# Candidate stages ahead of the dense chunks, stored split panels and stride-4 gate matmuls in a one-core encoder block

## The chip, the core and the metric

The kernel runs on one core of one Trainium2 chip. The metric is the device time of one execution in microseconds (us), lower is better. The time before is 3102.21 us, the median of 3 runs (3095.23 to 3104.54).

## What is computed

One residual block over 1024 tokens of width 1024, in f32. A mixer with 8 softmax heads and 8 stick-breaking heads comes first, then a PEER layer: every token picks, for each of 8 heads, 16 of 16384 single-neuron experts by product keys, and sums their outputs.

```python
query = (ht @ w_query).reshape(t, PEER_HEADS, 2, PEER_HALF)
sub_scores = jnp.einsum('thpd,hpkd->thpk', query, sub_keys)
half_vals, half_idx = lax.top_k(sub_scores, PEER_TOPK)
cand = (half_vals[:, :, 0, :, None] + half_vals[:, :, 1, None, :]).reshape(t, PEER_HEADS, 256)
top_vals, top_pos = lax.top_k(cand, PEER_TOPK)
experts = i1 * PEER_N_KEYS + i2
gates = jax.nn.softmax(top_vals, axis=-1)
...
act = jax.nn.gelu(jnp.einsum('td,thkd->thk', xb, expert_down[eb])) * gb
y = jnp.einsum('thk,thkd->td', act, expert_up[eb])
```

## The kernel before, in words

The 8 token tiles (128 tokens each) form two blocks. Block A holds tiles 0 to 4, block B tiles 5 to 7. The program has two parts.

**The front** runs, for both blocks, the projections, the attention, and then three steps. `post` (L774) is the output projection with w_out, `post_b` the second norm and transpose, and `route` (L825) the query projection with w_q and the top 16 of each half. Matrix products with f32 accuracy are done with split operands: a weight panel of 128x1024 is split into a high part (`wh`, ScalarE, L336) and a low part (`wl`, VectorE, L342), and `mm3` (L353) issues three matmuls for each piece. The class `Panels` (L316) loads a panel (L328), splits it and hands it out. `post` and `route` take 8 panels of w_out and 16 of w_q: 24 for block A, and the same 24 again for block B. The generator `cands` (L907) makes from eight rows of top-16 lists the final experts and gates. It is a chain of small VectorE operations with 12 yields; block A has five such stages, block B three (they are collected in `b.rest`).

The 5 tiles of block A are computed **densely**: all 16384 experts for all tokens, multiplied by a gate matrix that is zero except at the chosen experts. For tiles 0 and 1 the gate matrix is made by GpSimd: `scatter` (L1004) issues 256 indirect DMAs that add 128 gates each into the DRAM tensors `gds` (one for each of the two tiles, in turn). For tiles 2 to 4 it is made by TensorE: `gbuild` (L1016) builds one-hot tiles (VectorE L1033 and L1046, ScalarE L1042), multiplies them (L1050, 768 matmuls of 128x128), evicts them on ScalarE (L1052, 96 times) into `gt`, and stores that to DRAM as `gd` (L1055).

**The dense part** (from L1226) runs 32 groups of 4 chunks of 128 experts. A chunk's down panel is split (`split_d`), multiplied (`gelu_s`, L1274), passed through Gelu (L1280) and multiplied by its gates (`mul_g`, L1282); then the group's up products run into 10 accumulators. The gates of a group are loaded by `loadg` (L1248) from `gds` and `gd`; for the first two groups these loads stand on GpSimd's queue.

The 3 tiles of block B are computed **sparsely** beside it: the generator `sparse` (L1181) first runs the three `cands` stages of block B (36 steps), then for each expert slot gathers 128 rows of `expert_down` or `expert_up` into one of 5 `ring` buffers with an indirect DMA on GpSimd (L1194, L1207) and multiplies them on VectorE (L1196, L1212). `pump(n)` advances this generator by n steps at fixed places of the dense loop; `PUMP_0` is how many steps are issued ahead of the first `split_d`.

The order: in the front a scheduler sets each engine's order from the program and a timing model. In the dense part VectorE, ScalarE and TensorE run in the order in which the code is written; the order on GpSimd and on SP, which issues all plain DMAs, is still the scheduler's.

Of the kernel before, what the change touches and what calls it, by code (L numbers as in the profile page):

```python
# [11 lines left out]
F32 = mybir.dt.float32  # L12
F32R = mybir.dt.float32r
# [3 lines left out]
AF = mybir.ActivationFunctionType  # L17
# [3 lines left out]
P = 128  # L21
T = 1024
D = 1024
# [24 lines left out]
O2B = 2  # L48
WB = 3
UB = 4  # L50
PUMP_0 = 7
PUMP_C = 2
PUMP_U = 5
PUMP_V = 2
# [51 lines left out]
def tile_kernel(ctx: ExitStack, tc: tile.TileContext, x, ccol, w_ada, badac, bgt2, gcols, w_in, w_f, bf_, gout,  # L106
                w_out, w_q, keysT, edown, eup, wdense, gfin, out, dbg=None, stop=None):
    nc = tc.nc
    V, S, G, PE = nc.vector, nc.scalar, nc.gpsimd, nc.tensor
    dma = nc.sync.dma_start  # L110
# [3 lines left out]
    dram = ctx.enter_context(tc.tile_pool(name="dram", bufs=1, space=bass.MemoryType.DRAM))  # L114
# [38 lines left out]
    qsp = dram.tile([8, 3, P, T], F32R, name="qsp")  # L153
    ksp = dram.tile([8, 2, P, T], F32R, name="ksp")
    vsp = dram.tile([8, P, T], F32, name="vsp")
    gd = dram.tile([NPT * P // SB, P, NE * SB], F32, name="gd")
    gds = [dram.tile([NE * P * P, 1], F32, name="gds%d" % i) for i in range(NSC)]
    pidx = cst.tile([P, 1], F32, name="pidx")
# [2 lines left out]
    class Block:  # L161
        def __init__(self, t0, parts):
            self.t0, self.parts = t0, []
            i0 = 0
            for n in parts:
                self.parts.append((i0, n))
                i0 += n
            self.nt = i0
            self.ht = i0 * P
            self.nk = (t0 + i0) * P  # L170
            self.nq = 2 if t0 else 1
# [67 lines left out]
    def defer(fn, n=1):  # L239
        t_ = [n, fn]  # L240
        late.append(t_)
        return t_

    def force(t_):
        if t_ in late:
            late.remove(t_)
            t_[1]()
# [27 lines left out]
    def mrg(*streams, bg=()):  # L275
        live = [[q[0], float(q[1]), 0.0, q[2] if len(q) > 2 else 0] for q in streams + tuple(bg)]
        side = [q[0] for q in bg]
        need = len(streams)
        while need:
            for q in sorted(live, key=lambda q: q[2] / q[1]):  # L280
                c = adv(q)
                if c is None or c >= 0:
                    break
            assert c is None or c >= 0
            if c is None:
                live.remove(q)
                need -= not any(q[0] is g for g in side)
                continue
            q[2] += c
            tick(c)  # L290
            step()
        while late:
            late.pop(0)[1]()
        lead.clear()
# [17 lines left out]
    def split(dst_h, dst_l, src):  # L312
        S.activation(dst_h, src, AF.Copy)
        V.tensor_sub(dst_l, src, dst_h.bitcast(F32))

    class Panels:  # L316
        def __init__(self, pool, srcs, bufs=3, eng=V):
            self.eng = eng
            self.pool, self.src, self.bufs = pool, list(srcs), bufs
            self.ld, self.sp = [], []  # L320
            for _ in range(bufs - 1):
                self.load()
            self.split()

        def load(self):
            if self.src:
                w = self.pool.tile([P, D], F32, name="wf", tag="wf", bufs=self.bufs)
                dma(w, self.src.pop(0))  # L328
                self.ld.append(w)

        def split(self):
            if self.ld:
                w = self.ld.pop(0)
                wh = self.pool.tile([P, D], F32R, name="wh", tag="wh", bufs=2)
                wl = self.pool.tile([P, D], F32R, name="wl", tag="wl", bufs=2)
                S.activation(wh, w, AF.Copy)  # L336

                def low():
                    if self.eng is G:
                        G.tensor_sub(wl, w, wh.bitcast(F32))  # L340
                    else:
                        V.tensor_sub(wl, w, wh.bitcast(F32))  # L342

                self.sp.append((wh, wl, defer(low, LW)))
                self.load()

        def get(self):
            wh, wl, t_ = self.sp.pop(0)
            force(t_)
            self.split()  # L350
            return wh, wl

    def mm3(pt, wh, wl, hh, hl, cs, m=P, k0=0, k1=KD):  # L353
        for kd in range(k0, k1):
            c = slice(kd * m, (kd + 1) * m)
            PE.matmul(pt, wl[:, c], hh[:, kd, cs], start=kd == 0, stop=False)  # L356
            PE.matmul(pt, wh[:, c], hl[:, kd, cs], start=False, stop=False)  # L357
            PE.matmul(pt, wh[:, c], hh[:, kd, cs], start=False, stop=kd == KD - 1)  # L358
# [657 lines left out]
    def gbuild(ti, gp, alloc):  # L1016
        tp = alloc()
        for n, s_ in enumerate(cols3[ti]):
            PE.transpose(tp[:, n * P:(n + 1) * P], s_, identf)
        ib = gp.tile([P, 2, P], BF, name="ib", tag="ib", bufs=2)  # L1020
        S.activation(ib, tp[:, :2 * P].rearrange("p (n t) -> p n t", n=2), AF.Copy)
        gT = gp.tile([P, P], F32, name="gT", bufs=2)
        S.activation(gT, tp[:, 2 * P:3 * P], AF.Copy)
        io4 = gp.tile([P, P, 4], BF, name="io4", bufs=1)
        if ti == NSC:
            V.tensor_copy(io4, iof[:, :, None].to_broadcast([P, P, 4]))
            gio.append(io4)
        iob = gio[0][:, None].to_broadcast([P, 2, P, 4])

        def onehot(n, t):  # L1030
            o = gp.tile([P, 2, P, 4], BF, name="ob%d" % n, tag="ob", bufs=3)
            ids = ib[:, n, t:t + 8].rearrange("p (q t) -> p q t", t=4)[:, :, None, :]
            V.tensor_tensor(o, iob, ids.to_broadcast([P, 2, P, 4]), OP.is_equal)  # L1033
            return o.rearrange("p q i t -> p q t i")

        for sb in range(P // SB):
            gt = gp.tile([P, NE, SB], F32, name="gt", tag="gt", bufs=GTB)
            for q in range(SB // 8):
                t = sb * SB + q * 8
                e2 = onehot(1, t)  # L1040
                o2 = gp.tile([P, 2, 4, P], F32, name="o2", tag="o2", bufs=O2B)
                S.activation(o2, e2, AF.Copy)  # L1042
                e1 = onehot(0, t)
                o1 = gp.tile([P, 2, 4, P], F32, name="o1", tag="o1", bufs=O1B)
                gs = gT[:, t:t + 8].rearrange("p (q t) -> p q t", t=4)[:, :, :, None]
                V.tensor_tensor(o1, e1, gs.to_broadcast([P, 2, 4, P]), OP.mult)  # L1046
                for q2 in range(2):
                    pg = alloc()
                    for r in range(4):
                        PE.matmul(pg[:, r * P:(r + 1) * P], o2[:, q2, r], o1[:, q2, r], start=True, stop=True)  # L1050
                    c_ = q * 8 + q2 * 4
                    S.activation(gt[:, :, c_:c_ + 4].rearrange("p i t -> p t i"), pg.rearrange("p (t i) -> p t i", i=P),  # L1052
                                 AF.Copy)
                    yield GBC
            dma(gd[(ti - NSC) * (P // SB) + sb], gt.rearrange("p i t -> p (i t)"))  # L1055

# [2 lines left out]
    st_hpa, st_pw, st_hpb, st_xp, st_ad, st_at, st_s3, st_gp = [ExitStack() for _ in range(8)]  # L1059

    def pool(stack, name, bufs=1, **kw):
        return stack.enter_context(tc.tile_pool(name=name, bufs=bufs, reuse_waits="tile", **kw))
# [8 lines left out]
    def xtile(p_, b, name):  # L1071
        return p_.tile([P, b.nt, D], F32, name=name, tag="xr")
# [35 lines left out]
    am[0], ax[0] = ALS[0]()  # L1108
    s3p = pool(st_s3, "s3p", side="right")
    wop = [w_out[j] for j in range(KD)] + [w_q[j] for j in range(16)]  # L1110
    opan = Panels(s3p, wop, bufs=2)
    mrg((post(bA, mixA, lambda: xtile(xp, bA, "x1A"), opan), 60, HPB), (ad3, AD3), bg=((pp, PP3), (zr, ZR3)))
    rA = chain(post_b(bA), route(bA, opan))
    mrg((pp, PP4), (ad5, 10), bg=((rA, TOT_RA, HPC), (zr, 20)))
    for st_ in (st_ad, st_hpb, st_pw, st_xp):
# [8 lines left out]
    am[0], ax[0] = ALS[2]()  # L1124
    soft_rs[0] = RS2
    mb = pool(st_at, "mb")
    opan = Panels(s3p, wop, bufs=2)
    hp_[0] = pool(st_hpa, "hpc", 2)
    gp = pool(st_gp, "gp")
    mrg((chain(post(bB, mixB, lambda: xtile(mb, bB, "x1B"), opan), post_b(bB), route(bB, opan)), 150),  # L1130
        (chain(*[gbuild(ti, gp, ptp) for ti in range(NSC, ND)]), TOT_G))
    for st_ in (st_gp, st_hpa, st_at, st_xp, st_s3):
        st_.close()
# [192 lines left out]
    def sp_(n):  # L1326
        pump(n)
# [4 lines left out]
    def nextload():  # L1332
        i1 = next(loads, None)
        if i1 is not None:
            ready.append(load(i1))

    for _ in range(WB):
        nextload()
    sp_(PUMP_0)
    nxt = ready.pop(0)  # L1340
# [103 lines left out]
```

## Time and profile before

| | |
|---|---|
| median of 3 runs | 3102.21 us (3095.23 to 3104.54) |
| the profiled execution, its own time | 3110.21 us |
| its span | 3108.4 us |
| TensorE busy | 2856.6 us, 92% |
| VectorE busy | 2562.2 us, 82% |
| ScalarE busy | 1213.7 us, 39% |
| GpSimd busy | 1605.1 us, 52% |
| mean granted TensorE clock | 0.965 |
| HBM read, written | 721.52 MB, 77.76 MB |

Busy times are sums over the whole span, and an engine's share is an average over stages that differ. Times in the trace are counted from the span's start, and L12 is line 12 of the kernel before. PE is TensorE, DVE VectorE, ACT ScalarE, POOL GpSimd, and SP the engine that issues plain DMAs. A line that names a wait gives the idle time just before an instruction and what ended it; a row of a view of waits gives who waited for whom, the total, how often, and the longest.

### The profile page before, as it was taken

What the parts mean: (1) busy time and instruction counts of PE and PEld (TensorE: products, weight loads), DVE (VectorE), ACT (ScalarE), POOL (GpSimd) and SP (SyncE); (2) the same over time, 40 slices, a digit from 0 to 9 for tenths busy, and PEclk for the clock granted to TensorE, in tenths of its full rate; (3) what the DMA queues carried; (4) which work ended last, traced back from release to release, by engine and by line L of the source; (5) the groups of instructions that cost most, each with busy time, mean ns of one, the idle gap of its engine ahead of it and who ended that gap; (6) DMA issues with size and microseconds to landing.
All of it is one profiled execution on the core that took longest, in us unless ns stands there. A gap on an engine that the chain in (4) does not pass through costs nothing.

```text
span 3108.4 us, 47296 instructions
## 1 busy us (share of the span) xinstructions
PE 2856.6 (92%) x17213; PEld 2642.6 (85%) x17213; DVE 2562.2 (82%) x5226; ACT 1213.7 (39%) x2098; POOL 1605.1 (52%) x1092
## 2 busy tenths in 40 slices
PE   5899998998988895379999999999999999999997
PEld 4899998988888794379989989899898988999986
DVE  6677655899987697388988999899899988989986
ACT  5566645446677873131222213222122231222312
POOL 0000000077777666426566776665676756657771
PEclk9999999998989998689999999999999999999999
DMA  7999433455535555449999999999999999999995
GB/s 251 287 343 280 135 125 120 138 126 135 123 66 129 157 154 138 92 149 342 357 338 336 343 343 334 353 338 356 328 349 346 336 347 347 349 337 330 351 326 191
DMA packets 360313, 802.43 MB, mean 258 GB/s; under 512 B 66168, under 2 KB 174736, under 8 KB 358544
## 3 DMA queue, kind: packets, MB, share of 16 engines
q0 software_dynamic: 150352, 413.34, 39.4%
q1 hardware_dynamic: 209728, 386.08, 36.6%
q8 instruction: 135, 2.21, 0.3%
q14 instruction: 98, 0.80, 0.1%
HBM read 721.52 MB, written 77.76 MB: 257 GB/s over the span
## 4 chain that ended last, share of the span: by engine, by line
PE 29%; POOL 19%; issue 19%; DMA 17%; DVE 12%; ACT 2%; SPq 0%; POOLq 0%; DVEq 0%; ACTq 0%
POOL gds L1012 7%; DMA gds<-g,e 7%; POOL ring L1194 6%; DMA ring<-in_eup,e 6%; POOL ring L1207 5%; PE sp L356 3%; PE sp L357 3%; PE sp L358 3%; DMA wa<-in_w_ada 2%; PE po L1303 2%; PE po L1304 2%; PE po L1305 2%; PE proj L356 2%; PE proj L357 2%; PE proj L358 2%
## 5 line engine op out<-in xcount | busy, mean ns | idle before, releaser
L356 PE MATMUL sp<-hT,dl 128*128 128x320 f32 x2048 | 636.0, 311 | 86.3 <-ACT ge L1280 77.5
L1207 POOL DMA_INDIRECT ring<-in_eup,e x384 | 578.9, 1508 | 256.5 <-DVE sacc L1212 172.4
L1194 POOL DMA_INDIRECT ring<-in_edown,e x384 | 503.9, 1312 | 394.5 <-DVE ring L1196 230.8
L1012 POOL DMA_INDIRECT gds<-g,e x256 | 471.4, 1841 | 321.0 <-DVE i L867 136.4
L357 PE MATMUL sp<-hT,dh 128*128 128x320 f32 x2048 | 635.3, 310 | 0.0
L358 PE MATMUL sp<-hT,dh 128*128 128x320 f32 x2048 | 635.3, 310 | 0.0
L1212 DVE SCALAR_TENSOR_TENSOR sacc<-ring,sdot,sacc 128x1024 f32<-128x1024 f32 x381 | 489.3, 1284 | 56.0 <-DMA ring<-in_eup,e 51.4
L1196 DVE SCALAR_TENSOR_TENSOR ring<-ring,sx 128x1024 f32<-128x1024 f32 x384 | 460.9, 1221 | 67.9 <-DMA ring<-in_edown,e 67.0
L356 PEld LDWEIGHTS sp<-hT,dl 128*128 128x128 f32 x2048 | 386.9, 189 | 88.7 <-ACT ge L1280 79.9
L1269 ACT ACTIVATE uh<-wfu 128x1024 fp32r<-128x1024 f32 x128 | 134.8, 1053 | 672.5 <-PE po L1305 672.5
L357 PEld LDWEIGHTS sp<-hT,dh 128*128 128x128 f32 x2048 | 386.9, 189 | 1.2
L358 PEld LDWEIGHTS sp<-hT,dh 128*128 128x128 f32 x2048 | 386.7, 189 | 0.0
L1303 PE MATMUL po<-ul,ch 128*128 128x512 f32 x768 | 302.6, 394 | 17.5 <-DVE accB L1312 10.1
L1280 ACT ACTIVATE ge<-sp 128x320 f32<-128x320 f32 x256 | 110.5, 433 | 499.4 <-PE sp L358 492.6
L1304 PE MATMUL po<-uh,ch 128*128 128x512 f32 x768 | 300.6, 391 | 0.0
L1305 PE MATMUL po<-uh,cl 128*128 128x512 f32 x768 | 300.3, 391 | 0.0
L1304 PE MATMUL pers<-uh,ch 128*128 128x512 f32 x512 | 199.6, 390 | 0.0
L1303 PE MATMUL pers<-ul,ch 128*128 128x512 f32 x512 | 199.5, 390 | 0.0
L1305 PE MATMUL pers<-uh,cl 128*128 128x512 f32 x512 | 199.2, 389 | 0.0
L302 POOL TENSOR_TENSOR i<-ms,mhalf 128x4 f32<-128x4 f32 (+1 forms) x16 | 22.4, 1400 | 331.0 <-DVE ms L300 331.0
L1303 PEld LDWEIGHTS po<-ul,ch 128*128 128x128 f32 x768 | 145.1, 189 | 53.8 <-DVE accB L1312 16.0
L1305 PEld LDWEIGHTS po<-uh,cl 128*128 128x128 f32 x768 | 145.2, 189 | 30.5
(306 smaller groups left out, 6519.4 us busy)
## 6 DMA issues: line engine op xcount, KB each, us to landing
wfd<-in_wdense SPq DMA_DIRECT2D x128, 512.0 KB
wfu<-in_wdense SPq DMA_DIRECT2D x128, 512.0 KB
wa<-in_w_ada SPq DMA_DIRECT2D x96, 256.0 KB
wf<-in_w_in SPq DMA_DIRECT2D x48, 512.0 KB
gd<-gt SPq DMA_DIRECT2D x12, 2048.0 KB
g<-gd SPq DMA_DIRECT2D x30, 768.0 KB
gds<-zt SPq DMA_DIRECT2D x32, 512.0 KB
wf<-in_w_q SPq DMA_DIRECT2D x32, 512.0 KB
```

The costliest lines, as they stand in the source:

```text
L356: PE.matmul(pt, wl[:, c], hh[:, kd, cs], start=kd == 0, stop=False)
L357: PE.matmul(pt, wh[:, c], hl[:, kd, cs], start=False, stop=False)
L358: PE.matmul(pt, wh[:, c], hh[:, kd, cs], start=False, stop=kd == KD - 1)
L1012: G.indirect_dma_start(out=gds[i], out_offset=off, in_=b.g[:, c_:c_ + 1], in_offset=None, compute_op=OP.add)
L1194: G.indirect_dma_start(out=r, out_offset=None, in_=edown, in_offset=bass.IndirectOffsetOnAxis(ap=bs.e[:, c_:c_ + 1], axis=0))
L1196: (V.scalar_tensor_tensor(r, r, 1.0, sx, op0=OP.mult, op1=OP.mult, accum_out=s_[:, j:j + 1]))
L1207: G.indirect_dma_start(out=r, out_offset=None, in_=eup, in_offset=bass.IndirectOffsetOnAxis(ap=bs.e[:, c_:c_ + 1], axis=0))
L1212: (V.scalar_tensor_tensor(acc, r, s_[:, j:j + 1], acc, op0=OP.mult, op1=OP.add))
L1269: S.activation(k.uh, k.wfu, AF.Copy)
L1303: PE.matmul(po, k.ch[:, tcs], k.ul[:, ds_], start=c == 0 and (gi == 0 or not per), stop=False)
L1304: PE.matmul(po, k.ch[:, tcs], k.uh[:, ds_], start=False, stop=False)
L1305: PE.matmul(po, k.cl[:, tcs], k.uh[:, ds_], start=False, stop=c == CG - 1 and (gi == NG - 1 or not per))
```

## The change

Three edits.

1. `PUMP_0` goes from 7 to 44: all 36 candidate steps of block B and the first 8 sparse slots are issued before the first dense split.
2. Block A's `Panels` also stores each split panel (`wh` and `wl`, 512 KB each) to a DRAM tensor `wsp`; block B reads them back through a new class `Kept`, with three buffers, and neither loads nor splits its own.
3. The 128x128 gate matmuls of `gbuild` write every fourth column of their PSUM tile, so that the eviction reads and writes runs of four.

```diff
-PUMP_0 = 7
+PUMP_0 = 44
...
+    wsp = dram.tile([24, 2, P, D], F32R, name="wsp")
...
     class Panels:
-        def __init__(self, pool, srcs, bufs=3, eng=V):
-            self.eng = eng
+        def __init__(self, pool, srcs, bufs=3, eng=V, keep=None):
+            self.eng, self.keep = eng, keep and list(keep)
...
                 S.activation(wh, w, AF.Copy)
+                kp = self.keep.pop(0) if self.keep else None
 
                 def low():
                     if self.eng is G:
                         G.tensor_sub(wl, w, wh.bitcast(F32))
                     else:
                         V.tensor_sub(wl, w, wh.bitcast(F32))
+                    if kp is not None:
+                        for n_, t_ in enumerate((wh, wl)):
+                            dma(kp[n_].bitcast(F32), t_.bitcast(F32))
...
+    class Kept:
+        def __init__(self, pool, srcs, bufs=3):
+            self.pool, self.src, self.bufs, self.ld = pool, list(srcs), bufs, []
+            for _ in range(bufs - 1):
+                self.load()
+
+        def load(self):
+            if self.src:
+                src = self.src.pop(0)
+                t = [self.pool.tile([P, D], F32R, name=n_, tag=n_, bufs=self.bufs) for n_ in ("wh", "wl")]
+                for n_, t_ in enumerate(t):
+                    dma(t_.bitcast(F32), src[n_].bitcast(F32))
+                self.ld.append(t)
+
+        def get(self):
+            self.load()
+            return self.ld.pop(0)
...
                     for r in range(4):
-                        PE.matmul(pg[:, r * P:(r + 1) * P], o2[:, q2, r], o1[:, q2, r], start=True, stop=True)
+                        PE.matmul(pg.rearrange("p (i t) -> p i t", t=4)[:, :, r], o2[:, q2, r], o1[:, q2, r],
+                                  start=True, stop=True)
                     c_ = q * 8 + q2 * 4
-                    S.activation(gt[:, :, c_:c_ + 4].rearrange("p i t -> p t i"), pg.rearrange("p (t i) -> p t i", i=P),
-                                 AF.Copy)
+                    S.activation(gt[:, :, c_:c_ + 4], pg.rearrange("p (i t) -> p i t", t=4), AF.Copy)
...
-    opan = Panels(s3p, wop, bufs=2)
+    opan = Panels(s3p, wop, bufs=2, keep=[wsp[j] for j in range(24)])
...
-    opan = Panels(s3p, wop, bufs=2)
+    st_s3.close()
+    opan = Kept(pool(st_s3, "s3k", side="right"), [wsp[j] for j in range(24)], 3)
```

How the order moves. First VectorE where the dense part begins (`dl` is the low part of a down panel, `ul` of an up panel, `e` the expert numbers, rows with `bq`, `bi`, `cur` are candidate steps, `ring,sdot` a sparse slot). Before:

```order
L867 MAX_INDEX i_12774<-v_12773,sr 128x8
L865 MATCH_REPLACE sr<-v_12773,scs 128x128
L955 SCALAR_TENSOR_TENSOR bq<-pos,bq 128x128
L1264 TENSOR_TENSOR dl<-wfd,dh 128x1024 x2
L865 MATCH_REPLACE sr<-v_12773,scs 128x128
L866 MAX v_12773<-sr 128x8 x2
L1272 TENSOR_TENSOR ul<-wfu,uh 128x1024
L959 CAST bi<-af 128x128
```

With the change (its lines are 24 higher there):

```order
L1017 SCALAR_TENSOR_TENSOR tm<-af,bq 128x128
L1024 CAST e_4710<-tm 128x128
L1220 SCALAR_TENSOR_TENSOR ring,sdot<-ring,sx 128x1024 x8
L1288 TENSOR_TENSOR dl<-wfd,dh 128x1024 x2
L1296 TENSOR_TENSOR ul<-wfu,uh 128x1024
L1220 SCALAR_TENSOR_TENSOR ring,sdot<-ring,sx 128x1024 x2
L1310 TENSOR_TENSOR ge<-ge,gg 128x256
```

The first two dense splits stood in the middle of block B's first candidate stage; now they stand behind all three stages and behind eight sparse slots.

GpSimd's order is the same in both kernels. Here it is with the change, from the end of the scatters:

```order
L1035 DMA gds_108<-g_4709,e_4708 2097152x1
L1035 DMA gds_109<-g_4709,e_4708 2097152x1
L1277 DMA gg<-gds_108 128x512
L1277 DMA gg<-gds_109 128x512
...
L1279 DMA g_14191<-gd 128x12x128
L1213 DMA sx<-h2d 128x1024
L1218 DMA ring<-in_edown,e 128x1024
```

Nothing moved on this queue: the gate loads of the first two groups stand behind the last scatter, and the first sparse gather behind them.

Last, SP's queue in block A's `route`, while block B is still being projected. Before:

```order
L545 DMA ksp<-pka 128x384
L545 DMA ksp<-pkb 128x384
L328 DMA wf<-in_w_in 128x1024
L328 DMA wf<-in_w_q 128x1024
L328 DMA wf<-in_w_in 128x1024
```

With the change:

```order
L568 DMA ksp<-pka 128x384
L568 DMA ksp<-pkb 128x384
L329 DMA wf<-in_w_in 128x1024
L347 DMA wsp<-wh 128x1024
L347 DMA wsp<-wl 128x1024
L329 DMA wf<-in_w_q 128x1024
L329 DMA wf<-in_w_in 128x1024
```

Two stores of 512 KB now precede the load of each further panel. In block B's part each load of a raw panel gives way to two loads from `wsp`.

## Rows read from the trace of the kernel before

**Rows 1.** Page: TensorE by slices of 77.7 us; waits in 1210:1300 (VectorE), 1200:1300 (TensorE).

```profile
PE   5899998998988895379999999999999999999997
...
DVE ge L1286 <- DMA gg<-gds: 62.9, 1, 62.9
PE sp L356 <- ACT ge L1280: 69.8, 1, 69.8
```

**Rows 2.** GpSimd's timeline around the last scatter: start, us, engine, line, operation [idle before].

```profile
1276.34 1.55 POOL L1012 DMA_INDIRECT gds<-g,e  x1 [0.31 <-issue]
1278.20 1.55 POOL L1012 DMA_INDIRECT gds<-g,e  x1 [0.30 <-issue]
1279.90 0.63 POOL L1253 DMA_DIRECT2D gg<-gds  x1 [0.15 <-issue]
...
1285.06 0.59 POOL L1189 DMA_DIRECT2D sx<-h2d  x1
1339.73 1.04 POOL L1194 DMA_INDIRECT ring<-in_edown,e  x1 [54.08 <-DVE tv L935]
1370.69 1.55 POOL L1194 DMA_INDIRECT ring<-in_edown,e  x1 [29.92 <-DVE e L1001]
1372.55 1.95 POOL L1194 DMA_INDIRECT ring<-in_edown,e  x1 [0.30 <-issue]
1374.81 1.64 POOL L1194 DMA_INDIRECT ring<-in_edown,e  x1 [0.30 <-issue]
```

**Rows 3.** Four stretches: PE, PEld, DVE, ACT, POOL busy (count), clock, DMA share, GB/s.

```profile
624.00:797.00 173.00, 154.32 (x1000) 146.46 (x999) 169.14 (x763) 90.47 (x182) 125.11 (x70) 0.92 0.56 133
797.00:943.00 146.00, 131.16 (x914) 120.59 (x914) 131.79 (x393) 105.18 (x213) 107.59 (x60) 0.89 0.39 79
943.00:1210.00 267.00, 224.37 (x1508) 212.52 (x1507) 221.30 (x681) 203.09 (x269) 181.64 (x93) 0.95 0.57 162
1222.00:1278.00 56.00, 3.29 (x23) 3.02 (x21) 0.00 (x0) 0.00 (x0) 46.74 (x31) 0.57 0.22 0
```

**Rows 4.** GpSimd's timeline near the front's end, and its scatter waits over the whole span.

```profile
1203.09 1.61 POOL L1012 DMA_INDIRECT gds<-g,e  x1 [1.25 <-issue]
1205.00 1.55 POOL L1012 DMA_INDIRECT gds<-g,e  x1 [0.30 <-issue]
1210.71 2.70 POOL L1012 DMA_INDIRECT gds<-g,e  x1 [4.16 <-DMA gds<-g,e]
...
POOL gds L1012 <- DMA gds<-g,e: 120.8, 70, 6.1
```

**Rows 5.** Groups of instructions in 943:1210, count, then busy us and mean ns.

```profile
L1012 POOL DMA_INDIRECT gds<-g,e x93 | 183.2, 1970 | 82.2 <-DMA gds<-g,e 61.5 <-issue 20.8
L1052 ACT ACTIVATE gt<-tp 128x512 f32<-128x512 f32 x96 | 98.7, 1118 | 29.5 <-PE tp L1050 17.9 <-DMA gd<-gt 8.9 <-issue 2.5
L342 DVE TENSOR_TENSOR wl<-wf,wh 128x1024 fp32r<-128x1024 f32 x22 | 27.6, 1254 | 8.8 <-ACT wh L336 7.0 <-ACT of L809 1.6
L336 ACT ACTIVATE wh<-wf 128x1024 fp32r<-128x1024 f32 x22 | 23.3, 1058 | 0.0
L856 ACT ACTIVATE scs<-proj 128x384 f32<-128x384 f32 x16 | 8.0, 502 | 9.8 <-DVE sr L865 7.3 <-PE proj L854 1.3 <-issue 1.2
```

**Rows 6.** Splits on VectorE and panel loads in 624:797.

```profile
L342 DVE TENSOR_TENSOR wl<-wf,wh 128x1024 fp32r<-128x1024 f32 x14 | 17.2, 1226 | 0.0
...
wf<-in_w_in SPq DMA_DIRECT2D x3, 512.0 KB
```

**Rows 7.** VectorE's timeline: first and last step of one candidate stage of block B.

```profile
1304.98 0.73 DVE L923 TENSOR_TENSOR cand<-v 128x128 f32<-128x128 f32 x5
1338.13 0.23 DVE L1001 CAST e<-tm 128x128 int32<-128x128 f32 x1
```

**Rows 8.** Timeline, TensorE's first dense matmul, and ScalarE's first Gelu of groups 0, 2, 3.

```profile
1208.99 0.63 PE L356 MATMUL sp<-hT,dl 128*128 128x320 f32 x1 [7.33 <-DVE dl L1264]
...
1214.76 0.44 ACT L1280 ACTIVATE ge<-sp 128x320 f32<-128x320 f32 x1 [9.86 <-PE sp L358]
...
1419.22 0.44 ACT L1280 ACTIVATE ge<-sp 128x320 f32<-128x320 f32 x1 [4.49 <-PE sp L358]
...
1474.60 0.44 ACT L1280 ACTIVATE ge<-sp 128x320 f32<-128x320 f32 x1 [4.49 <-PE sp L358]
```

**Rows 9.** VectorE's timeline, second and third sparse slot.

```profile
1376.33 1.23 DVE L1196 SCALAR_TENSOR_TENSOR ring<-ring,sx 128x1024 f32<-128x1024 f32 x1 [0.69 <-DMA ring<-in_edown,e]
1380.76 1.23 DVE L1196 SCALAR_TENSOR_TENSOR ring<-ring,sx 128x1024 f32<-128x1024 f32 x1 [1.33 <-DMA ring<-in_edown,e]
```

**Rows 10.** TensorE's gate matmuls on the timeline, one merged run.

```profile
1102.28 1.87 PEld L1050 LDWEIGHTS tp<-o,o 128*128 128x128 f32 x16
1102.38 1.95 PE L1050 MATMUL tp<-o,o 128*128 128x128 f32 x16
```

## Prediction

> **What bounds the kernel now.** I read the slices of the page first: TensorE is 90% busy or more from the nineteenth slice (1400 us) on, and in the three before it, from 1166, only 50, 30 and 70% [rows 1]. Two limits follow, one behind the other. In the dense part it is TensorE itself: groups 2 and 3 begin 1474.60 - 1419.22 = 55.4 us apart [rows 8], and nothing in this change touches the work of a group. So a gain or a loss must show in when the dense part gets going. The waits in that hole say what it is for [rows 1]: VectorE stands 62.9 us before the first gate multiplication, for the load of `gg`, and TensorE behind it for 69.8 us. That load stands on GpSimd's queue behind the last of the 256 scatters, which is issued at 1278.20, and goes out at 1279.90 [rows 2]. So the front's engines are through by about 1210, and **the scatter chain sets the start.** Work that VectorE, ScalarE or TensorE save in the front only lengthens the hole.
>
> What paces the chain is read from four stretches [rows 3]. With no plain traffic (1222 to 1278) one scatter takes 1278.20 - 1276.34 = 1.86 us [rows 2]. At 79 GB/s it takes 146/60 = 2.43, at 133 GB/s 173/70 = 2.47, at 162 GB/s 267/93 = 2.87. How it does so stands in [rows 4]: the scatter at 1210.71 waited 4.16 us for an earlier one to land, since those to one tensor go one after another; such waits sum to 120.8 us. Traffic makes landings late. The chain is not short of work: these waits and the issue gaps are all that 943 to 1210 shows [rows 5].
>
> **The change, part by part.**
>
> *Stored panels, engines.* Block B loses 24 splits: 24 x 1.254 = 30 us of VectorE and 24 x 1.058 = 25 us of ScalarE [rows 5]. I cost both at nothing on the path: the scatters cover them, by about 70 us (1210 to 1280). The front may end some 35 us earlier.
>
> *Stored panels, traffic.* Block A writes 24 x 1.05 = 25 MB more and block B reads 12.6 MB more. Only what moves after the first scatter counts. Of the 14 splits after 624, 5 belong to block B's projection (3 loads seen, two panels in flight), so 9 are block A's [rows 6]: 9.4 MB over 173 us, +55 GB/s. How much that slows a scatter the trace shows only by its stretches, so I bound it: the flattest pair of [rows 3] (79 to 133 GB/s) gives 0.0007 us per GB/s, the steepest (0 to 162) 0.0063. I take the middle, 0.0035: 2.47 + 0.19 = 2.66 us, 65 scatters in place of 70. The 5 that are left are made up at the end at 1.86: **+9 us** (bounds +1 and +16). For block B, 12.6 MB more in 232 us in place of 267 makes (43 + 12.6)/232 = 241 GB/s; at the slope between its neighbours (79 to 162: 0.0053) a scatter takes 2.87 + 0.42 = 3.29. Then 232/3.29 = 70.5 are done there and 35/1.86 = 18.8 in the quiet 35 us that follow: 89.3 of 93, so 3.7 x 1.86 = +7. If the front ends no earlier, it is 267/3.12 = 85.6 and +14. I take **+10**; the bounds are -10 (flat slope, earlier end: 232/2.92 + 18.8 = 98.2 done) and +16. SP's queue carries the 48 stores; each waits for the same low split as the load behind it waited for before, so I add nothing for that.
>
> *Candidates ahead.* One stage takes 1338.13 + 0.23 - 1304.98 = 33 us with some dense work inside [rows 7], two and a half are left when the front ends, so about 75 us. They now run in the hole, beside the last scatters. A scatter's own issue is 1.55 us with VectorE idle [rows 2] and 1.97 on average beside a busy one [rows 5]. The last 59 us at 1.86 + 0.42 in place of 1.86 hold 26 scatters, not 32: at most +11, at least 0; I take **+5**. VectorE's lost splits could give back 0.42 x 93 x 30/221 = 5; I leave that in the lower bound.
>
> *Eight slots ahead of the first split.* These wait on VectorE for gathers that stand on GpSimd behind the last scatter, and everything dense is queued behind them; TensorE's first matmul waits for `dl`. So the two chunks that TensorE now does before the hole are no longer done ahead. Against the same last scatter: GpSimd is free at 1285.65 after `sx`; eight gathers at 1372.55 - 1370.69 = 1.86 us start until 1298.7 [rows 2]; a gather is used 1376.33 - 1372.55 = 3.8 to 1380.76 - 1374.81 = 6.0 us after its start [rows 2, 9], so the last slot begins at 1302.5 to 1304.7. With 1.2 for it and 1.2 for `dl`, TensorE starts at 1305 to 1307, and the first Gelu follows 1214.76 - 1208.99 = 5.8 us later [rows 8], at 1311 to 1313. Before, group 2 begins at 1419.22; two groups back that is 1308.4. So what the hole took before (two chunks ahead, but then candidate stages in between the chunks) and what it takes now nearly cancel: **+4 us**, between 0 and +15 (if gathers come at the 3 us at which ring buffers come free later).
>
> *Stride-4 gate matmuls.* ScalarE's eviction takes 1118 ns for 512 columns; 384 contiguous ones take 502 [rows 5], so I estimate 650 and a saving of 96 x 0.47 = 45 us (0 if the stride was not its cost). It lies before the hole: nothing. A matmul takes 1.95/16 = 0.12 us now [rows 10]; strided writes are not in this trace. In the front TensorE has 267 - 224 = 43 us free [rows 3] and the hole adds 70, so up to 113/768 = 0.15 us more for each costs nothing; with the 24 us of later scatters, 0.18. I take no loss.
>
> The sparse stream ends about 37 steps earlier; the tail then waits for TensorE's last groups as before: 0.
>
> Sum: 9 + 10 + 5 + 4 = +28 on the profiled execution's own 3110.21, so 3138. That execution lies 8 us above the median of 3102.21; against the median the forecast is **3130 us**, slower by 0.9%. Bounds: 1 - 10 - 5 + 0 = -14 and 16 + 16 + 11 + 15 = +58, so 3088 to 3160.
>
> **The rivals.** A difference of under 0.3% (9 us) cannot be told from none.
>
> *Earlier quiet, faster.* A loaded scatter costs about the same at any traffic, as 2.43 and 2.47 at 79 and 133 GB/s suggest. Then denser traffic costs nothing, and a front that ends 35 us earlier gives the chain a quiet stretch sooner: 35 us at 1.86 in place of 2.87 is 6.6 scatters, 12 us, and VectorE's lost splits give 5. With +1 and +4 the time is 3102 - 12 = 3090. It decides if traffic above 162 GB/s slows a scatter by less than 0.1 us. Against it speaks the step from 2.47 to 2.87.
>
> *A draw.* The two effects cancel, and the start costs its +4: 3095 to 3111.
>
> *Slow strided writes.* If each gate matmul took four times its 0.12 us, TensorE would get 768 x 0.37 = 281 us more; 137 of it is covered (43 + 70 + 24), and the front's end, no longer the scatters, would set the start: 3130 + 144 = 3274. It decides above 0.18 us more per matmul. The Trainium skill, page "SBUF — State Buffer", section "Door 1: The DMA port swizzle", says that any non-contiguous access to PSUM significantly slows matmuls, since a PSUM line holds two f32 values; it names no factor, and no run here shows one. By that rule at a factor of two the cover would still hide it, and at four this rival would be the result.
>
> That the change does not do what it says is excluded by the order: the three stages and eight slots do stand ahead.
>
> **How the numbers follow.** The later scatters: 0.55. The faster rival: 0.22. The draw: 0.19. Slow strided writes: 0.04. So faster 0.22, same 0.19, slower 0.59. The forecast's own range is 3112 to 3160. To hold 8 in 10 the range takes in the draw and most of the faster rival, and leaves out the strided one: 3086 to 3162.
>
> **What would show each step.** Right: the last scatter is issued later than 1278, near 1302; scatters in the stretches after 624 and after 943 at 2.6 to 3.3 us; the eight slots' waits on VectorE end just behind it, and TensorE's first dense matmul comes some 27 us after the last scatter; groups still 55.4 us apart. Wrong: a last scatter before 1270, a first dense matmul ahead of it, or group times that differ; a gate matmul run of 16 well above 1.95 us would point to the last rival.

## The result and the profile after

The changed kernel takes 3137.84 us, the median of 4 runs (3131.62 to 3143.17), against 3103.38 on the same chip: a ratio of 1.0108 [1.0085, 1.0131] (the brackets after a ratio are its 95% interval), **slower by 1.1%**. The forecast was 3130, within 3086 to 3162. The profiled execution took 3143.17 us, with a span of 3141.4; against the profiled execution before that is 33 us more.

| profiled execution | before | after |
|---|---|---|
| span, us | 3108.4 | 3141.4 |
| VectorE busy | 2562.2 | 2538.4 |
| ScalarE busy | 1213.7 | 1149.2 |
| HBM read, written, MB | 721.52, 77.76 | 734.11, 102.92 |
| last scatter issued at | 1278.20 | 1302.07 |
| first Gelu of group 2 | 1419.22 | 1450.79 |

VectorE lost 24 us of work and ScalarE 64, and the time grew. The traffic grew by the 25 MB and 12.6 MB that the prediction counted. The page's slices of TensorE (78.5 us each) show the hole that [rows 1] showed, now deeper: 10, 0 and 90% in the sixteenth to eighteenth slice, where it was 50, 30 and 70.

```profile
PE   5899998989988981099999999999999999999997
```

The waits of VectorE and TensorE in 1150:1360 (who waited for whom: us in total, times, longest) name other tiles than [rows 1]. VectorE now stands first for the first gather of the eight sparse slots, and TensorE for `dl`, the low part of the first down panel, which is queued behind those slots:

```profile
DVE ring L1220 <- DMA ring<-in_edown,e: 61.9, 4, 59.7
...
PE sp L379 <- DVE dl L1288: 140.2, 1, 140.2
```

The four stretches of [rows 3] again (PE, PEld, DVE, ACT, POOL busy with count, clock, DMA share, GB/s):

```profile
624.00:797.00 173.00, 154.47 (x1013) 146.20 (x1012) 170.02 (x770) 90.55 (x186) 113.07 (x63) 0.93 0.66 180
797.00:943.00 146.00, 131.76 (x909) 120.68 (x909) 130.23 (x380) 103.46 (x205) 108.29 (x58) 0.89 0.39 80
943.00:1210.00 267.00, 216.41 (x1492) 210.11 (x1490) 211.19 (x742) 144.07 (x246) 158.88 (x88) 0.92 0.66 205
1222.00:1278.00 56.00, 0.00 (x0) 0.00 (x0) 35.37 (x143) 6.74 (x8) 46.31 (x29) 0.50 0.20 1
```

The first stretch carries 180 GB/s in place of 133 and has 63 scatters in place of 70; the third 205 in place of 162, and 88 in place of 93. One scatter takes 173/63 = 2.75, 146/58 = 2.52, 267/88 = 3.03 and, in the quiet, 56/29 = 1.93 us. GpSimd's timeline (start, us, operation, idle before) shows the end of the chain and what follows:

```profile
1302.07 1.55 POOL L1035 DMA_INDIRECT gds<-g,e  x1 [0.30 <-issue]
1303.77 0.63 POOL L1277 DMA_DIRECT2D gg<-gds  x1 [0.15 <-issue]
...
1309.17 0.59 POOL L1213 DMA_DIRECT2D sx<-h2d  x1
1310.07 1.04 POOL L1218 DMA_INDIRECT ring<-in_edown,e  x1 [0.30 <-issue]
...
1315.16 0.93 POOL L1218 DMA_INDIRECT ring<-in_edown,e  x1 [0.30 <-issue]
1321.53 1.74 POOL L1218 DMA_INDIRECT ring<-in_edown,e  x1 [5.44 <-DVE ring L1220]
```

VectorE's timeline, first and eighth slot and the two splits behind them:

```profile
1320.03 1.23 DVE L1220 SCALAR_TENSOR_TENSOR ring<-ring,sx 128x1024 f32<-128x1024 f32 x1 [59.66 <-DMA ring<-in_edown,e]
...
1331.05 1.23 DVE L1220 SCALAR_TENSOR_TENSOR ring<-ring,sx 128x1024 f32<-128x1024 f32 x1 [0.78 <-DMA ring<-in_edown,e]
...
1332.20 2.36 DVE L1288 TENSOR_TENSOR dl<-wfd,dh 128x1024 fp32r<-128x1024 f32 x2
```

And TensorE's first dense matmul, then ScalarE's first Gelu of groups 0, 1 and 2 (compare [rows 8]):

```profile
1333.48 0.64 PE L379 MATMUL sp<-hT,dl 128*128 128x320 f32 x1 [140.20 <-DVE dl L1288]
...
1340.02 0.44 ACT L1304 ACTIVATE ge<-sp 128x320 f32<-128x320 f32 x1 [77.15 <-PE sp L381]
...
1395.40 0.44 ACT L1304 ACTIVATE ge<-sp 128x320 f32<-128x320 f32 x1 [1.97 <-PE sp L381]
...
1450.79 0.44 ACT L1304 ACTIVATE ge<-sp 128x320 f32<-128x320 f32 x1 [4.49 <-PE sp L381]
```

The groups are 55.39 us apart, as before. Group 2 starts 31.6 us later than before; the span is 33.0 longer. So nearly all of the loss is there when the dense part gets going, and it has two pieces: the last scatter (+23.9) and the way from it to group 2 (148.7 in place of 141.0 us, +7.7).

### The profile page after: what moved, and what is told of

It is laid out like the page before. It is cut to its first block, busy times and chain, and to the rows that moved or that the text cites. A ratio compares the mean times of both kernels' runs of the same rounds, so it can differ in the third digit from the quotient of the medians.

```text
span 3141.4 us, 47353 instructions
## 1 busy us (share of the span) xinstructions
PE 2848.1 (91%) x17213; PEld 2642.4 (84%) x17213; DVE 2538.4 (81%) x5202; ACT 1149.2 (37%) x2068; POOL 1592.5 (51%) x1092
## 3 DMA queue, kind: packets, MB, share of 16 engines
HBM read 734.11 MB, written 102.92 MB: 266 GB/s over the span
## 5 line engine op out<-in xcount | busy, mean ns | idle before, releaser
L1231 POOL DMA_INDIRECT ring<-in_eup,e x384 | 587.2, 1529 | 247.4 <-DVE sacc L1236 170.7
L1218 POOL DMA_INDIRECT ring<-in_edown,e x384 | 497.1, 1294 | 337.6 <-DVE ring L1220 261.7
L1035 POOL DMA_INDIRECT gds<-g,e x256 | 458.9, 1793 | 358.4 <-DMA gds<-g,e 162.0
## 6 DMA issues: line engine op xcount, KB each, us to landing
g<-gd SPq DMA_DIRECT2D x30, 768.0 KB, 15.8
```

The costliest lines, as they stand in the source:

```text
L1035: G.indirect_dma_start(out=gds[i], out_offset=off, in_=b.g[:, c_:c_ + 1], in_offset=None, compute_op=OP.add)
L1218: G.indirect_dma_start(out=r, out_offset=None, in_=edown, in_offset=bass.IndirectOffsetOnAxis(ap=bs.e[:, c_:c_ + 1], axis=0))
L1231: G.indirect_dma_start(out=r, out_offset=None, in_=eup, in_offset=bass.IndirectOffsetOnAxis(ap=bs.e[:, c_:c_ + 1], axis=0))
```

## The experiments

**Each part by itself.** Six kernels take the parts apart. Without the reads and the stores of split panels:

```diff
-    opan = Panels(s3p, wop, bufs=2, keep=[wsp[j] for j in range(24)])
+    opan = Panels(s3p, wop, bufs=2)
...
-    st_s3.close()
-    opan = Kept(pool(st_s3, "s3k", side="right"), [wsp[j] for j in range(24)], 3)
+    opan = Panels(s3p, wop, bufs=2)
```

> The changed kernel without the stored panels (block B splits its own again, nothing is stored); candidates, eight slots and stride-4 matmuls stay. Theory (the extra traffic makes the scatters late, the eight slots cost a little): the last scatter is issued near 1280 again, the first Gelu 38 us behind it as in the changed kernel, so 3103 + 2 + 8 = 3113 us. Rival (the scatters are late because the candidate stages run beside them): the last scatter stays near 1302, and the time near 3138.

Measured: ratio 1.0064 [1.0047, 1.0081] (3127.66 against 3107.51), last scatter at 1277.07. Taking the panels away brings the last scatter back to where it was, though not the time, which was expected at 3113: what is left is 20 us by the medians and 10 by the profiled executions.

The panels alone (7 steps ahead, the old matmul and eviction):

```diff
-PUMP_0 = 44
+PUMP_0 = 7
...
-    S.activation(gt[:, :, c_:c_ + 4], pg.rearrange("p (i t) -> p i t", t=4), AF.Copy)
+    S.activation(gt[:, :, c_:c_ + 4].rearrange("p i t -> p t i"), pg.rearrange("p (t i) -> p t i", i=P), AF.Copy)
```

> The kernel before with the stored panels alone (7 steps ahead, matmuls and eviction as before). Theory: the traffic alone makes the last scatter some 20 us later, near 1298, and the time is 3103 + 20 = 3123 us. Rival (traffic is not the cause): last scatter near 1278 or, with VectorE's splits gone, a little earlier; 3095 to 3105 us.

Measured: 1.0058 [1.0035, 1.0080]; last scatter at 1294.34. The stored panels alone make the kernel slower by 20 us (3127.88 against 3107.51).

Stores by block A, but block B loads and splits its own panels:

```diff
-    st_s3.close()
-    opan = Kept(pool(st_s3, "s3k", side="right"), [wsp[j] for j in range(24)], 3)
+    opan = Panels(s3p, wop, bufs=2)
```

> The changed kernel in which block A stores its split panels but block B does not read them: it loads and splits raw panels as before. Theory: the stores after the first scatter cost 9 us, the reads the rest, so the last scatter is issued near 1288 (between the 1277 without stored panels and the 1302 of the change), fewer scatters than 70 in 624 to 797 and about 92 in 943 to 1210. Rival (reads alone make the scatters late): last scatter near 1278 and 69 or 70 scatters in 624 to 797.

Measured: 1.0064 [1.0046, 1.0082]; last scatter at 1291.86. That is between the kernels without panels and the changed one, and the stretches went as expected: 65 scatters in 624:797 and 93 in 943:1210. The medians do not show the stores: this ratio is the 1.0064 that the kernel without any stored panel has.

The stride alone (the edit of the first kernel, and `PUMP_0 = 7`), then the same again in another set of runs:

> The kernel before with the stride-4 gate matmuls and their eviction alone. Theory: ScalarE saves about 50 us ahead of the hole, and nothing of it reaches the end: last scatter near 1278, ratio to the kernel before within 0.3% of 1. Rival (strided writes slow the matmuls): a run of 16 gate matmuls takes well over 1.95 us; the ratio leaves 1 only if the front ends behind the scatters. Second rival (the shorter front lets the scatters finish earlier): last scatter before 1270, ratio 0.997 or less.

> The kernel before with stride 4 alone, a second time, for the spread. If its 0.3% is real: ratio 1.002 to 1.004 again, and the trace shows a last scatter later than 1279 or a group 2 more than 141 us behind it. If not: within 0.2% of 1.

Measured: 1.0031 [1.0018, 1.0044] and 1.0020 [1.0007, 1.0033], 10 runs each. The changed kernel without the stride, with the old matmul and the old eviction, in the second set:

```diff
-    PE.matmul(pg.rearrange("p (i t) -> p i t", t=4)[:, :, r], o2[:, q2, r], o1[:, q2, r],
-              start=True, stop=True)
+    PE.matmul(pg[:, r * P:(r + 1) * P], o2[:, q2, r], o1[:, q2, r], start=True, stop=True)
```

> The changed kernel with matmuls and eviction of the gates as before. If the stride costs 0.3%: ratio 1.008 in place of 1.011. If it costs nothing: 1.011. If the 45 us that it takes off ScalarE helped: over 1.011.

Measured: 1.0090 [1.0071, 1.0110], against 1.0108 [1.0085, 1.0131] with it. And the kernel before once more, for a second profile of it:

> The kernel before once more, one look, for the spread of the last scatter from one execution to the next: between 1274 and 1290, group 2 141 us behind it.

Measured: 3103.54 us, one run; last scatter at 1271.1 (1278.2 in the first profile), 3 us below the expected range; group 2 comes 141.7 us behind it, as expected.

**The scatter chain in all of these.** One row of each trace gives its length, from the first of the 256 scatters to the last (durations in ns are minimum, median, maximum). Of the stride alone, then the panels alone:

```profile
L1035 POOL DMA_INDIRECT gds<-g,e x256: 1541/1553/6226, 620.7 to 1276.2; - x128
```

```profile
L1035 POOL DMA_INDIRECT gds<-g,e x256: 1540/1552/4862, 621.2 to 1294.3; - x128
```

The table holds this length for every kernel with 256 scatters, and the time from the last scatter to group 2's first Gelu.

| panels | stride 4 | steps ahead | chain, us | to group 2 |
|---|---|---|---|---|
| raw | no | 7 | 654.4, 649.3 | 141.0, 141.7 |
| raw | no | 34 | 647.8 | 125.2 |
| raw | yes | 7 | 655.5, 658.6 | 141.5, 140.6 |
| raw | yes | 34 | 659.3 | 117.2 |
| raw | yes | 36 | 664.5 | 125.6 |
| raw | yes | 44 | 656.9 | 148.0 |
| stored, not read | yes | 44 | 667.8 | 146.9 |
| stored | no | 7 | 673.1 | 141.4 |
| stored | no | 44 | 667.5 | 147.3 |
| stored | yes | 36 | 672.2 | 125.4 |
| stored | yes | 44 (the change) | 678.9 | 148.7 |

Two traces of one setting differ by up to 5 us, and settings that differ in the steps ahead alone by up to 9, so the means count. Without panels and stride the chain is 650.5 (3 traces), with the stride 659.0 (5), with the stores too 667.8 (1), with the panels and no stride 670.3 (2), with all of it 675.6 (2). So panels as a whole cost 17 to 20 us, and **the stride about 8** without the panels (the two ranges, 647.8 to 654.4 and 655.5 to 664.5, do not meet, though by 1 us only). With the panels the stride's part, 5 us, is not shown, since those ranges meet. The panels' part divides into about 9 us for the stores and 8 for the reads by a single trace, the one with stores and no reads. For the stores there is more: in 624:797, where their traffic falls, all five traces with them hold 63 to 66 scatters, at 176 to 181 GB/s, and all eight without hold 69 to 72, at 132 to 135; 5 scatters at 1.86 us are some 10 us. For the reads there is not: in 943:1210, with the stride, 88 and 91 scatters with them stand among the 88 to 93 without.

The candidate stages ahead show no cost on the chain: 656.9 with 44 steps ahead against 657.0 (two traces) with 7, and the other traces with 34 to 44 steps lie from 5.6 us below to 7.5 us above those with 7 that are otherwise alike. The right column goes by the steps ahead, whatever the panels and the stride: 140.6 to 141.7 with 7, 146.9 to 148.7 with 44, 125.4 and 125.6 with 36. With 34 its two values differ by 8, for a reason given below.

The medians agree with these pieces within 6 us. Panels and 44 steps ahead make 19.8 + 6.5 = 26.3 us, and the changed kernel without the stride is 3133.69 - 3107.39 = 26.3 above the kernel before. The stride alone makes 8.5 on the chain, and 8.9 and 5.3 in its two comparisons. The widest gaps are 44 steps with the stride (8.5 + 6.5 = 15 by the pieces, 20 by the medians) and the changed kernel with 36 steps, below (25.1 - 15.8 = 9 by the pieces, 3.5 by the medians, at most 8 by the interval). Part of this lies behind group 2: from its first Gelu to the end of the span the traces with 36 steps take 1686 and 1688 us, those with 44 take 1691 to 1693.

**Do the scatters set the start?** This kernel leaves out half of them.

```diff
-        for k in range(16):
+        for k in range(0, 16, 2):
```

> The changed kernel with every second of the 16 slots of a head left out of the scatter (128 of the 256 scatters; the gates of tiles 0 and 1 are incomplete). Theory (the scatter chain sets the start): the last scatter is issued before 1010, the dense part starts when the candidate stages and eight slots are through, with its first Gelu near 1270 in place of 1340, and the time is near 3138 - 65 = 3073 (3060 to 3090). Rival (the front or the candidate stages set the start anyway): 3125 or more.

Measured, one run: 3085.95 us, inside the expected range; the last scatter is issued at 977.4, the first Gelu comes at 1282.53, where the changed kernel has 1340.02. The chain is what the dense part waits for. The first Gelu is later than expected, and the time with it: behind the scatters stands the next limit, VectorE's own front and candidate stages, whose last step is at 1259.28, and the eight slots behind them.

**Fewer steps ahead.** 36 steps are the three candidate stages without a sparse slot; in the changed kernel, then also without the panels:

```diff
-PUMP_0 = 44
+PUMP_0 = 36
```

> The changed kernel with 36 steps ahead in place of 44: the candidate stages alone, no sparse slot before the first dense split. Theory: the last scatter stays at 1302, but two chunks are multiplied ahead of it again, and the dense part restarts some 24 us closer to it than in the changed kernel: 3138 - 20 = 3118 us (3108 to 3125). Rival (the slots cost nothing, since the gathers must be done in any case): 3133 to 3140 us.

> 36 steps ahead and stride-4 matmuls, but no stored panels. Theory: the last scatter near 1280, the candidate stages hidden in the hole, two chunks ahead of it: faster than the kernel before by what its stages cost between the chunks, about 16 us: 3088 us. Rival (the stages between the chunks cost nothing before): 3103 us.

Measured: 1.0015 [1.0004, 1.0026] and 0.9961 [0.9948, 0.9975]. Against 44 the way from the last scatter to group 2 falls from some 148 to 125.5 us. The changed kernel so comes to 3110.96 us, inside the theory's range, and without the panels the kernel is faster than before by 11 us (3096.26 against 3107.51), between the theory's 3088 and the rival's 3103. With the 8 slots taken away, the first dense matmul is no longer behind the last scatter. In the second of these kernels TensorE's timeline has it at 1270.83, 15.6 us ahead of the last scatter at 1286.46:

```profile
1270.83 0.64 PE L379 MATMUL sp<-hT,dl 128*128 128x320 f32 x1 [78.43 <-DVE dl L1287]
```

34 steps, two fewer than the stages have; without panels but with the stride, and as the only edit to the kernel before:

> Without stored panels, stride-4 matmuls, and 34 steps ahead: the last two candidate steps take the places that sparse slots 1 and 2 had behind the first chunk, so that no gather is awaited ahead of the first gate multiplication. Theory: the third chunk starts as close to the last scatter as in the kernel before (first Gelu of it 22 us behind the last scatter, not 29 as with 36 steps), with no candidate stage between the chunks: 6 us better than with 36 steps, ratio 0.994. Rival: the two slots only move to the next chunk and hold it up there; ratio 0.996 as with 36.

> The kernel before with 34 steps ahead as its one edit. If the stride-4 gate matmuls cost the 0.3% that their run alone showed in its times, this is 0.3% faster than the run with 34 steps and stride 4: ratio 0.993. If they cost nothing and that 0.3% was the spread of the last scatter between runs: 0.996, as with them. Last scatter near 1279 in both cases, group 2 begins 117 us behind it.

Measured: 0.9959 [0.9944, 0.9975] and 0.9964 [0.9948, 0.9979]. The 0.994 that the theory had for the first lies just outside its interval, the rival's 0.996 inside. The two are one result, though their last scatters stand 9.6 us apart (1279.28 and 1269.66). By the expectation on record that speaks for a stride that costs nothing here. Read afterwards, their waits on VectorE tell why it would not show. With the stride the first chunk is multiplied early, and its gates are waited for:

```profile
DVE ge L1309 <- DMA gg<-gds: 17.3, 1, 17.3
```

Without it no such wait is left; the first dense matmul is at 1278.05, behind the last candidate steps on VectorE, when the gates are already being loaded, and group 2 starts at 1394.91, the other kernel's at 1396.49. Once no slot stands ahead of the first split, the chain and the candidate stages end together, and a few microseconds on either no longer show. **One number, `PUMP_0 = 34`, in the kernel before is the simplest of the faster versions here:** 3093.54 us against 3107.39, and no other version is shown to be faster than it.

## Why the prediction was right

*What bounds the kernel.* Right. The front's engine savings were worth nothing, the work of a group stayed at 55.4 us, and the loss shows in when the dense part starts.

*Stored panels, engines: 0.* Right, and the savings are in the rows. In 943:1210 no split of a panel is left. The groups there (count, busy us and mean ns, idle before and what ended it) show the eviction, which the stride changed, at 601 ns where [rows 5] has 1118:

```profile
L1035 POOL DMA_INDIRECT gds<-g,e x88 | 159.1, 1808 | 108.4 <-DMA gds<-g,e 89.4 <-issue 15.6 <-ACT gt L1076 3.5
...
L1076 ACT ACTIVATE gt<-tp 128x512 f32<-128x512 f32 x96 | 55.9, 601 | 65.2 <-PE tp L1073 52.2 <-DMA gd<-gt 12.9
```

ScalarE's gain went into waiting: 52.2 us for TensorE's gate tiles, where it was 17.9 before.

*Stored panels, traffic: stores +9, reads +10.* The sum of 19 was right: 16.6 to 19.8 us on the chain; how it divides between stores and reads is less sure, as said above. The pace after 624 was forecast as 2.66 us a scatter and came as 2.75, though only 13 of the 48 stores, 6.8 MB, fell there and not the 9.4 MB of the sum (whose lower bound for the stores comes to +2, not +1). After 943 the sum had 3.29 us a scatter until the front ends at 1175, and 1.86 behind that: 70.5 and 18.8 scatters. The trace has 72 issued before 1175 (3.22 us each) and 15 after. There the row above shows two effects against each other. A scatter's own issue fell from 1970 to 1808 ns, as the prediction's lower bound allowed for the splits that VectorE loses: in the four traces with reads it is 1708 to 1808 in the mean, in the nine others 1855 to 1981. The waits for landings rose from 61.5 us to 89.4 and took more than that. In the kernel before, of the 92 scatters issued in 943:1210, the 73 that overlap a two-input VectorE operation of the gate build or of a split (L1033, L1046, L342) by over 0.2 us take 2.07 us in the mean, the other 19 take 1.58. The Trainium skill, page "SBUF — State Buffer", section "Who interferes with whom", says that a VectorE instruction with two SBUF inputs contends with a GpSimd instruction that reads SBUF; these issue times agree with it, if issuing a scatter counts as such a read, which no run here separates. The longer landing is a cost that this rule does not speak of.

*Candidates beside the last scatters: +5.* Mis-sized: the chain shows none. Of 25 scatters issued between 1212 and 1262, beside the candidate stages, 17 still took 1.55 us and only three took 2.47, all three beside one long operation (a COPY_PREDICATED of 128x1024), so this work does not slow an issue as the front's work did, from which the 0.42 us was taken.

*Eight slots ahead: +4.* The mechanism was right, its size was +6.5 (means), or 7.7 in the profiled pair. The first dense matmul came 31.4 us after the last scatter, not 27. The step that was off is a gather's time to its use. The 3.8 to 6.0 us pair each slot of [rows 9] with a gather one place too late. The gathers are used in order, and the one of 1339.73 [rows 2] belongs to the first slot:

```profile
1372.47 1.22 DVE L1196 SCALAR_TENSOR_TENSOR ring<-ring,sx 128x1024 f32<-128x1024 f32 x1
```

So the second slot (1376.33) used the gather of 1370.69 and the third (1380.76) that of 1372.55: 5.6 and 8.2 us. With these the same sum puts the first dense matmul 28.5 to 31.1 us behind the last scatter. In the changed kernel the first slot began at 1320.03, 10 us after its gather's start, and the sixth gather waited 5.44 us for one of the five ring buffers, which the sum's eight gathers in a row leave out; the sixth to eighth were used 5.4 to 6.2 us after their start.

*Stride 4: 0.* The reason held, and the value did not. An unbroken run of 16 gate matmuls still takes 1.95 us as in [rows 10] (24 such runs in the trace before, 26 after):

```profile
1085.63 1.95 PE L1073 MATMUL tp<-o,o 128*128 128x128 f32 x16
```

So the rival of slow strided writes is out; what the Trainium skill's page "SBUF — State Buffer", section "Door 1: The DMA port swizzle", says of non-contiguous PSUM access slowing matmuls does not show in these rows. Yet the stride costs the scatter chain some 8 us where the panels are raw. The place shows when the scatters are counted through. From the 131st to the 191st, issued between some 940 and 1130 while the gate matmuls run, three traces without the stride take 164 to 168 us and five with it 173 to 185; over the last 65 they take 165 to 167 and 152 to 159, so a part comes back. In 943:1210 the waits for landings are 64.3 us in the mean without the stride and 70.2 with it, but these ranges meet (60.3 to 71.1 and 62.8 to 75.2). Why scatters come later when ScalarE evicts faster is not settled; no run varied the stores of the gate tiles.

*The rivals.* The earlier quiet came: in 1175:1195 the DMA engines moved 7 GB/s, where it was 190 before. TensorE's front itself ended only some 8 us earlier, at 1193. The quiet did not pay, since the denser traffic ahead of it did slow the scatters. The sum, 9 + 8 + 0 + 6.5 and some 5 to 8 for the stride, is 28 to 32 against the forecast 28 and the 31.6 of group 2's start. That it comes so close is in part luck: the stride and the slots, forecast too low, stand against the reads and the candidates, forecast too high.

## What to carry to other kernels

When one chain on one queue sets a start, price every byte and instruction by what it does to that chain; busy time saved elsewhere only lengthens the wait. Work that is pulled ahead of a start should be only what can run before that start: here 34 or 36 candidate steps fill a hole and gain 11 to 15 us, and eight more steps, which need a load behind the chain, turn that into a loss. A small term is measured across several traces of each setting: single traces of the same chain differ by 5 us here.

## What the runs showed of the hardware

- The same eviction of 512 f32 columns by ScalarE takes 601 ns where SBUF is written in runs of four, 1118 ns where neighbouring elements go to separate places [rows 5]. TensorE's f32 matmuls of 128x128 write PSUM with a 16-byte step at no visible cost: 1.95 us for 16 with the step and without it.
- Scatters that add into one tensor come more slowly beside plain traffic: in the same 173 us (624:797) 69 to 72 are issued at 132 to 135 GB/s (eight traces), 63 to 66 at 176 to 181 (five). The traffic is not all of it: in 943:1210 of the kernel before one takes 2.87 us at 162 GB/s, more than the 2.75 at 180 in 624:797 of the changed one.
- Issuing one such scatter takes GpSimd 1.55 us beside an idle VectorE [rows 2], and 2.07 in the mean beside the two-input VectorE operations of the gate build and the splits.
- A gather of 128 rows of 4 KB was used 10 us after its start when it was the first of five in a row behind the gate loads, and 5.4 to 6.2 us as the sixth to eighth; in the kernel before the second and third took 5.6 and 8.2.
